# Embedding product moved behind the output projection, parked in DRAM; whole tiles in the residual

## Chip, cores, metric

One core of a Trainium2 chip (trn2) runs the whole block in one launch. The metric is the device time of that launch in microseconds, the median of several runs.

## The reference

One layer (DEPTH = 1), 512 positions, 1024 channels, everything in float32; cut to what the change touches:

```python
hn = rms_norm(h, g_mix_pre)
# three mixers and three sigmoid gates, each from hn @ w_in
merged = gates[:, :, 0] * br_a + gates[:, :, 1] * br_b + gates[:, :, 2] * br_c
h = h + rms_norm(merged @ w_out, g_mix_post)
hn = rms_norm(h, g_ffn_pre)
f_gate, f_up = jnp.split(hn @ w_ffn_in, 2, axis=-1)      # 1024 -> 2 x 2816
f = (jax.nn.silu(f_gate) * f_up) @ w_ffn_out             # 2816 -> 1024
h = h + rms_norm(f, g_ffn_post)
h = h + jax.nn.sigmoid(h @ w_ple_gate) * (p @ w_ple)     # p: 512 x 256
```

`rms_norm(x, g)` is x * rsqrt(mean(x * x) + 1e-6) * g over the channels. The embedding's product is `p @ w_ple`; it depends on nothing that the block computes.

## The kernel before

Channels lie on the 128 partitions, positions (512, or halves of 256) along the free axis; 1024 channels are 8 k-blocks (KT), a hidden size of 2816 is 22 (FT). Each float32 operand is split into a high part (rounded to fp32r by ACT) and a low part (the rest, by DVE), and a product of one k-block is three matmuls into one PSUM bank: high weights by high and by low activations, low weights by high activations (`mm3`; `product` runs the k-blocks of one tile, `product_k_outer` one k-block for several tiles in turn). A tile of 8 k-blocks is thus 24 matmuls.

**Weights** come through class `Weights`: `add` lists the blocks in order, `_next` issues the load on SP (a `raw` tile of 512 KB, 3 buffers), the cast on ACT (`hi`) and the subtraction on DVE (`lo`); `get` takes the next block and `ahead(n)` prepares blocks until n are ready. A block with no tag goes into the 3 stream buffers of `hi` and of `lo`; one with a tag goes into slots of the activations' pool that are free at the time ("tm" 6, "br", "hn" and "cv" 8 each, named `w_hi` and `w_lo`). A slot is taken again when the last reader of what it held is done.

**Order.** All operations of PE, ACT and DVE go through the helper `InOrder.engine.call` (L69 before, L71 after), so every row of the profile has that line and is told apart by the names of its tiles. Inside `with order():` each engine keeps the order in which the program is written; elsewhere a scheduler orders it. An engine runs its instructions strictly in order. Seven PSUM banks ("ps") are shared by all products, an eighth ("pst", `ps_stat`) holds the statistics.

**The stages around the change**, in order: the conv branch's projection (`ps_br`); the **output projection** (`ps_o`, `mix_tile`): tiles 0 to 3 with all 512 positions, 4 to 7 first for the left half, then for the right, each copied with its gain to `o_all` and squared by ACT, the squares summed into `o_sums` by DVE (`add_mixed`). Then per half `inv_rms`: a matmul pair with `mean_mat` gives the mean, `rsqrt` is eight dependent DVE operations (`o_inv`). `Residual.tile(k)` follows: DVE multiplies `o_all` by it and adds to `h_all`; ACT writes the high part of the scaled `h_all` (`hg`), DVE the low part, which is held back until the next tile's multiplication is issued (`flush` for the last). `square_h` and `add_h` sum the squares of the new `h_all` into `h_sums`.

The first six **feed-forward blocks** (2 * `N_PAIR`, six banks `ps_f`) run with k outermost, left half, then right; ahead of the right half's last k (`STAT_H` = 7) comes the statistic of `h_sums` for `h_inv`. From then on each block is a whole tile (`ffn_tile`) and `swiglu` multiplies each pair by `h_inv` out of PSUM. ffn_out (`ps_fo`, 8 tiles of 22 k-blocks in cuts of 8, 7 and 7) ends with tile 7 in halves; `evacuate` copies to `o2_all` and sums squares into `f_sums`. Then come, before the change, the **embedding's product** (`ps_ple`, `ple_tile`: 8 tiles of 6 matmuls, its copies kept in SBUF in slots "br") and beside it the residual of the left half, then the **gate product** (`ps_pg`): four blocks (`N_LAST`) with k outermost by halves, the others as whole tiles but for the last, and `finish`: sigmoid, multiplication by the embedding, sum, and the write of the output.

```python
def residual_ffn(hs):
    y = t2("f_inv", H)
    inv_rms(f_sums[:, hs], y)
    return Residual(o2_all, hs, y, h2, lambda k: 1.0)
```

Of the kernel before, what the change touches and what calls it, by code (L numbers as in the profile page):

```python
# [8 lines left out]
F32 = mybir.dt.float32  # L9
# [3 lines left out]
AF = mybir.ActivationFunctionType  # L13
# [3 lines left out]
P = 128  # L17
# [64 lines left out]
def hybrid_block(  # L82
# [16 lines left out]
    stat = ctx.enter_context(tc.tile_pool(name="stat", bufs=2))  # L99
    psum = ctx.enter_context(tc.tile_pool(name="psum", bufs=7, space=PSUM))  # L100
# [106 lines left out]
    def mm3(out, wh, wl, xh, xl, first, last):  # L207
        pe.matmul(out, lhsT=wh, rhs=xh, start=first, stop=False)
        pe.matmul(out, lhsT=wh, rhs=xl, start=False, stop=False)
        pe.matmul(out, lhsT=wl, rhs=xh, start=False, stop=last)  # L210
# [4 lines left out]
    def product(ps, w, acts, hs=FULL, k0=0, last=True):  # L215

        hi, lo = w
        for i, a in enumerate(acts):
            mm3(ps[:, hs], blk(hi, i), blk(lo, i), a[:, 0, hs], a[:, 1, hs],
                k0 + i == 0, last and i == len(acts) - 1)  # L220
# [65 lines left out]
    N_HALF = 4  # L286
    N_PAIR = 3

    def add_mix(*blocks):
        for b in blocks:  # L290
            weights.add(w_mix[b])
# [401 lines left out]
    def mix_tile(n, w, hs):  # L693
        ps = bank("ps_o")
        product(ps, w, mix_T, hs)
        act_e.activation(out=o_all[:, n, hs], in_=ps[:, hs], func=AF.Copy, scale=col("g_mix_post", n))
        if n == 0:
            act_e.activation(out=o_sums[:, hs], in_=ps[:, hs], func=AF.Square)
            return None
        return square(ps[:, hs], "o_sq")  # L700
# [16 lines left out]
    lo_half, hi_half = HALVES  # L717
    with order():
        for n in range(KT - N_HALF):
            sq = mix_tile(n, weights.get(2), FULL)  # L720
            add_mixed(sq, n, FULL)
            weights.ahead((5, 7, 9, 10)[n])
        late = [weights.get(0) for _ in range(N_HALF)]
        blocks = [weights.get(0) for _ in range(2 * N_PAIR)]
        for i in range(N_HALF):
            n = KT - N_HALF + i
            add_mixed(mix_tile(n, late[i], lo_half), n, lo_half)
        sqs = []
        for i in range(N_HALF):
            n = KT - N_HALF + i  # L730
            sq = mix_tile(n, late[i], hi_half)
            if i == 0:
                y = t2("o_inv", H)
                inv_rms(o_sums[:, lo_half], y)
                res = Residual(o_all, lo_half, y, hg, ffn_gain)
            sqs.append((sq, n))
            for k in MIX_CUT[i]:
                res.tile(k)
                if sqs:
                    add_mixed(*sqs.pop(0), hi_half)  # L740
        res.flush()


        banks = [bank("ps_f") for _ in range(2 * N_PAIR)]
        product_k_outer(banks, blocks, hg, lo_half, range(STAT_A))
        for k in range(KT):
            square_h(k, lo_half)
            add_h(k, lo_half, nc.gpsimd)
        y = t2("o_inv", H)
        inv_rms(o_sums[:, hi_half], y)  # L750
        res = Residual(o_all, hi_half, y, hg, ffn_gain)
        for k in range(KT):
            res.tile(k)
            if k > 1:
                add_h(k - 2, hi_half, dve)
            if k:
                square_h(k - 1, hi_half)
        res.flush()
        square_h(KT - 1, hi_half)
        add_h(KT - 2, hi_half, dve)  # L760
        add_h(KT - 1, hi_half, dve)
# [53 lines left out]
    ple = [slot("br", f"ple{i}", F32) for i in range(4)]  # L815

    def ple_tile(n, w, p):
        ps = bank("ps_ple")
        for k in range(2):
            s = slice((2 * (n % 4) + k) * P, (2 * (n % 4) + k + 1) * P)  # L820
            ts = slice(k * T, (k + 1) * T)
            mm3(ps, w[0][:, s], w[1][:, s], p[0][:, ts], p[1][:, ts], k == 0, k == 1)
        act_e.copy(ple[n // 2][:, n % 2], ps)
# [12 lines left out]

    with order():
        ps = bank("ps_fo")
        halves = [bank("ps_fo") for _ in HALVES]
        ffn_out(ps, KT - 2, 0, weights.get(2))  # L840
        w = weights.get(1)
        for b, hs in zip(halves, HALVES):
            ffn_out(b, KT - 1, 0, w, hs)
        w = weights.get(1)
        ffn_out(ps, KT - 2, 1, w)
        weights.ahead(3)
        w = weights.get(2)
        ffn_out(ps, KT - 2, 2, w)
        p_w, w_ple_0 = weights.get(0), weights.get(0)
        weights.ahead(3)  # L850
        evacuate(ps, KT - 2, FULL)
        last = [weights.get(0), weights.get(0)]
        weights.ahead(3)
# [7 lines left out]
        product(halves[1], (hi[:, 3 * P:], lo[:, 3 * P:]), f_T[c0 + 3:c1], hi_half, c0 + 3, False)  # L861
        ffn_out(halves[1], KT - 1, 2, last[1], hi_half)
        evacuate(halves[1], KT - 1, hi_half)


        w_ple_1 = weights.get(0)
        blocks = [weights.get(0) for _ in range(2)]
        k = 0
        for n in range(KT):
            ple_tile(n, w_ple_1 if n >= 4 else w_ple_0, p_w)  # L870
            while n > 0 and k < PLE_CUT[n - 1]:
                res.tile(k)
                k += 1
            if n == PLE_SPLIT:
                weights.ahead(2)
        blocks += [weights.get(0) for _ in range(2)]
        res.flush()
        banks = [bank("ps_pg") for _ in range(N_LAST)]
# [5 lines left out]
        product_k_outer(banks, blocks, h2, lo_half, range(STAT_F, KT))  # L884
        product_k_outer(banks, blocks, h2, hi_half)
        weights.ahead(2)
        for n in range(N_LAST):
            finish(banks[n], n, FULL)
        for n in range(N_LAST, KT):
# [71 lines left out]
```

## Time and profile before

| | |
|---|---|
| median of 3 runs | 984.22 us (984.08 to 984.52) |
| the profiled execution | 983.63 us, of which span 981.9 us |
| PE, DVE, ACT, POOL busy | 973.8, 677.3, 346.1, 88.2 us |
| conv branch's projection | 468.68 to 512.20 us |
| output projection | 512.20 to 557.41 us |
| first six feed-forward blocks | 557.41 to 593.07 us |
| end of ffn_out, embedding's product, gate product | to 921.47, to 932.37, to the end |

The span is what the profiler records between the first and the last instruction of the core; the time of the execution is longer by what lies around it. A busy PE in these rows is one with matmuls in flight: their ends are modelled, so the start of one to the start of the next is the better measure of a matmul. Where an engine was idle ahead of an instruction, its row names in brackets for how long and which engine's work ended it.

### The profile page before, as it was taken

The page shows a single profiled execution, that of the slowest core. Times are in us where ns is not written, and L with a number is a line of the kernel's source. Part 1 is how long each engine was busy: PE and PEld are TensorE (multiplying, and loading weights), DVE is VectorE, ACT ScalarE, POOL GpSimd, SP SyncE. Part 2 cuts the span into 40 slices and gives each one's busy share as a digit, 9 for nine tenths or more (in the row PEclk, how much of TensorE's full clock was granted, in tenths as well). Part 3 has the DMA queues.
Part 4 walks back from the last instruction along what each step waited for, and adds up shares of the span by engine and source line. Part 5 has one row for each costly group of instructions (what it writes and reads, how often), then busy time and mean ns, then how long its engine had stood idle before and what let it go on. Part 6 is the DMA issues. An engine that isn't in the chain of part 4 may idle for free.

```text
span 981.9 us, 11718 instructions
## 1 busy us (share of the span) xinstructions
PE 973.8 (99%) x4682; PEld 819.2 (83%) x4682; DVE 677.3 (69%) x903; ACT 346.1 (35%) x483; POOL 88.2 (9%) x64
## 2 busy tenths in 40 slices
PE   9999999999999999999999999999999999999998
PEld 6788888788888878888888998888888888888897
DVE  7898789999988899957555787544444432223575
ACT  6422333332224332146435443323232322223442
POOL 4000004000013712160000010000000000000000
PEclk9999999999999999999999999999999999999999
DMA  6433331323322322332338112323322333334312
GB/s 233 137 108 107 109 106 65 107 69 104 107 81 81 101 103 86 105 110 68 126 96 272 62 38 74 104 90 104 98 96 93 98 91 104 92 92 139 109 43 86
DMA packets 30006, 100.53 MB, mean 102 GB/s; under 512 B 3456, under 2 KB 3968, under 8 KB 29952
## 3 DMA queue, kind: packets, MB, share of 16 engines
q1 hardware_dynamic: 29808, 99.75, 30.9%
q8 instruction: 36, 0.59, 0.2%
q14 instruction: 18, 0.15, 0.0%
q10 hardware_dynamic: 144, 0.04, 0.0%
HBM read 97.68 MB, written 2.10 MB: 102 GB/s over the span
## 4 chain that ended last, share of the span: by engine, by line
PE 88%; DVE 7%; issue 2%; DMA 1%; ACT 1%; SPq 0%; DVEq 0%; ACTq 0%
PE ps_f L69 25%; PE ps_br L69 13%; PE ps_fo L69 12%; PE ps_gate L69 12%; PE ps_ag L69 5%; PE ps_pg L69 5%; PE ps_o L69 5%; PE ps_z L69 4%; PE ps_nat L69 4%; DVE lo L69 2%; DVE acc L69 2%; PE ps_ple L69 1%; PE ps_pool L69 1%; DVE v_all L69 1%; DMA first_all<-in_w_first 1%
## 5 line engine op out<-in xcount | busy, mean ns | idle before, releaser
L69 ACT CAST hi<-raw 128x1024 fp32r<-128x1024 f32 (+3 forms) x158 | 162.5, 1030 | 456.3 <-PE ps_br L69 88.4
L69 DVE TENSOR_TENSOR lo<-raw,hi 128x1024 fp32r<-128x1024 f32 (+3 forms) x158 | 206.2, 1306 | 107.0 <-ACT hi L69 106.5
L69 DVE SCALAR_TENSOR_TENSOR acc<-h_conv,vec,acc 128x511 f32<-128x511 f32 (+14 forms) x240 | 183.3, 764 | 5.2
L69 PE MATMUL ps_f<-hg,hi 128*128 128x512 f32 (+1 forms) x624 | 184.5, 379 | 0.0
L69 PEld LDWEIGHTS ps_f<-hg,hi 128*128 128x128 f32 x624 | 115.1, 188 | 21.7
L69 PE MATMUL ps_gate<-hn,hi 128*128 128x512 f32 x384 | 119.6, 392 | 0.9 <-DVE gated L69 0.9
L69 PE MATMUL ps_f<-hg,lo 128*128 128x512 f32 (+1 forms) x312 | 118.0, 379 | 0.0
L69 PE MATMUL ps_fo<-f,hi 128*128 128x512 f32 (+1 forms) x396 | 111.0, 366 | 0.0
L69 PEld LDWEIGHTS ps_gate<-hn,hi 128*128 128x128 f32 x384 | 72.0, 188 | 17.1 <-DVE gated L69 1.3
L69 PEld LDWEIGHTS ps_fo<-f,hi 128*128 128x128 f32 x396 | 71.7, 189 | 12.2
L69 PE MATMUL ps_nat<-hi,hn 128*128 128x512 f32 x256 | 78.8, 390 | 0.0
L69 PE MATMUL ps_gate<-hn,lo 128*128 128x512 f32 x192 | 74.9, 390 | 0.0
L69 PE MATMUL ps_fo<-f,lo 128*128 128x512 f32 (+1 forms) x198 | 72.5, 366 | 0.0
L69 PEld LDWEIGHTS ps_f<-hg,lo 128*128 128x128 f32 x312 | 58.7, 188 | 11.0
L69 PEld LDWEIGHTS ps_nat<-hi,hn 128*128 128x128 f32 x256 | 48.1, 188 | 10.0
L69 DVE TENSOR_TENSOR f<-ps_f,h_inv 128x512 f32<-128x512 f32 x22 | 15.2, 690 | 56.5 <-PE ps_f L69 56.5
L69 PE MATMUL ps_nat<-lo,hn 128*128 128x512 f32 x128 | 49.9, 390 | 0.0
L69 PE MATMUL ps_ag<-hn,hi 128*128 128x512 f32 x160 | 49.6, 391 | 0.2 <-DVE sig L69 0.2
L69 PEld LDWEIGHTS ps_fo<-f,lo 128*128 128x128 f32 x198 | 37.4, 189 | 6.0
L69 PEld LDWEIGHTS ps_gate<-hn,lo 128*128 128x128 f32 x192 | 36.1, 188 | 7.5
L69 DVE TENSOR_TENSOR silu<-ps_f,h_inv 128x512 f32<-128x512 f32 x22 | 15.2, 690 | 36.0 <-PE ps_f L69 35.9
L69 PE MATMUL ps_br<-pool,hi 128*128 128x512 f32 x128 | 39.6, 389 | 0.0
(214 smaller groups left out, 1566.5 us busy)
## 6 DMA issues: line engine op xcount, KB each, us to landing
raw<-in_w_mix SPq DMA_DIRECT2D x90, 512.0 KB, 3.2
raw<-in_w_ffn_in SPq DMA_DIRECT2D x44, 512.0 KB, 3.3
raw<-in_w_ffn_out SPq DMA_DIRECT2D x16, 448.0 KB, 3.3
raw<-in_w_ffn_out SPq DMA_DIRECT2D x8, 512.0 KB, 3.5
raw<-in_w_ple_gate SPq DMA_DIRECT2D x8, 512.0 KB, 4.2
x_all<-in_xT SPq DMA_DIRECT2D x8, 256.0 KB, 6.4
h_all<-in_xT SPq DMA_DIRECT2D x4, 512.0 KB, 5.2
out_dram<-pg SPq DMA_DIRECT2D x7, 256.0 KB, 2.0
```

Source lines behind the costliest of these rows:

```text
L69: inst = op(*args, **kw)
```

## The change

- The output projection runs all 8 tiles whole. Behind it the 8 tiles of the embedding's product run; ACT copies each to a temporary tile `ple_out`, from which SP's queue writes it to a DRAM tile `ple_dram`. At the end of ffn_out four loads of 512 KB on SP's queue bring them back into slots "br" and "tm".
- The statistic of `o_sums` comes after the second embedding tile (`PLE_STAT`). The residual and the first six feed-forward blocks run in whole tiles; all additions into `h_sums` are DVE's (the left half's were POOL's).
- The weights for this (`pT`, two of `w_ple` in slots "tm", and the six feed-forward blocks) are listed between the output projection's blocks (`N_LATER`), with more blocks ahead (`AHEAD_OUT`). Feed-forward blocks 6 to 8, in slots "tm" before, now use the stream's buffers.
- ffn_out's tile 6 runs its last cut in halves, the left one first; the `f_sums` statistic of the left half now has four k-blocks of tile 6's right half ahead of it, not three of tile 7's. `evacuate` and `mix_tile` issue the square ahead of the copy.
- Two further gate blocks (`N_MORE`) run by halves, each on its own; the gate's blocks 0 to 3 go into slots "hn".

```diff
+AHEAD_OUT = (2, 2, 3, 4, 4, 5, 5, 4)
+N_LATER = (0, 0, 0, 1, 1, 1, 2, 4)
...
+    later = [(pT, "tm"), (w_ple[0], "tm"), (w_ple[1], "tm")]
+    later += [(w_ffn_in[b], "br" if b < 4 else None) for b in range(2 * FT)]
     for n in range(KT):
-        weights.add(w_mix[S_OUT + n], "tm" if KT - N_HALF <= n < KT - 1 else None)
-    for b in range(2 * FT):
-        weights.add(w_ffn_in[b], "br" if b < 4 else "tm" if 6 <= b < 9 else None)
+        add_mix(S_OUT + n)
+        for _ in range(N_LATER[n]):
+            weights.add(*later.pop(0))
+    for item in later:
+        weights.add(*item)
...
+    def ple_tile(n, w, p):
...
+        t = t2("ple_out")
+        act_e.copy(t, ps)
+        nc.sync.dma_start(out=ple_dram[:, n], in_=t)
...
     with order():
...
+        late = []
+        for n in range(KT):
+            w = weights.get(0)
+            weights.ahead(AHEAD_OUT[n])
+            late += [weights.get(0) for _ in range(N_LATER[n])]
+            add_mixed(mix_tile(n, w, FULL), n, FULL)
+        p_w, *w_ple_hl = late[:3]
+        for n in range(KT):
+            if n == PLE_STAT:
+                y = t2("o_inv")
+                inv_rms(o_sums, y)
+                res = Residual(o_all, FULL, y, hg, ffn_gain)
+            ple_tile(n, w_ple_hl[n // 4], p_w)
+        blocks = late[3:]
...
         for k in range(KT):
             res.tile(k)
             if k > 1:
-                add_h(k - 2, hi_half, dve)
+                add_h(k - 2, FULL, dve)
...
+        banks = [bank("ps_f") for _ in range(2 * N_PAIR)]
+        product_k_outer(banks, blocks, hg, FULL, range(STAT_H))
         weights.ahead(2)
-        product_k_outer(banks, blocks, hg, lo_half, range(STAT_A, KT))
-        product_k_outer(banks, blocks, hg, hi_half, range(STAT_H))
         inv_rms(h_sums, h_inv)
-        product_k_outer(banks, blocks, hg, hi_half, range(STAT_H, KT))
+        product_k_outer(banks, blocks, hg, FULL, range(STAT_H, KT))
...
+        ffn_out(ps, KT - 2, 2, w_last, lo_half)
+        evacuate(ps, KT - 2, lo_half)
...
         for c in (1, 2):
-            ffn_out(halves[0], KT - 1, c, last[c - 1], lo_half)
+            ffn_out(halves[0], KT - 1, c, late[c - 1], lo_half)
         evacuate(halves[0], KT - 1, lo_half)
-        c0, c1 = ffn_out_cuts[1]
-        hi, lo = last[0]
-        product(halves[1], (hi, lo), f_T[c0:c0 + 3], hi_half, c0, False)
+        c0, c1 = ffn_out_cuts[2]
+        product(ps, w_last, f_T[c0:c0 + 4], hi_half, c0, False, skip_group_check=True)
         res = residual_ffn(lo_half)
...
+        for i in range(4):
+            nc.sync.dma_start(out=ple[i], in_=ple_dram[:, 2 * i:2 * i + 2])
...
+        res.tile(0)
+        evacuate(ps, KT - 2, hi_half)
+        res.tile(1)
         evacuate(halves[1], KT - 1, hi_half)
...
         product_k_outer(banks, blocks, h2, lo_half, range(STAT_F))
+        more = [weights.get(1) for _ in range(N_MORE)]
         res = residual_ffn(hi_half)
```

How the change moves instructions at three places. **DVE around the inverse root of `h_sums`**: `h_sums`, `h_inv` and `rs_t` are rows of 512, `w_lo` and `lo` are the low parts of feed-forward weights. Before:

```order
L69 TENSOR_TENSOR h_sums<-h_sums,o_all 128x256 [waits DVE_49,Activation_49] x2
L69 TENSOR_TENSOR w_lo<-raw,w_hi 128x1024 [waits DMAHW6_49,Activation_49]
L69 TENSOR_TENSOR w_lo<-raw,w_hi 128x1024 [waits DMAHW7_49,Activation_49]
L69 TENSOR_SCALAR h_inv<-ps_stat 128x512 [waits PE_49]
L69 TENSOR_TENSOR rs_t<-h_inv 128x512 [waits DVE_49]
L69 SCALAR_TENSOR_TENSOR rs_t<-rs_t,ps_stat 128x512 [waits DVE_49]
L69 SCALAR_TENSOR_TENSOR h_inv<-rs_t,h_inv 128x512 [waits DVE_49]
L69 TENSOR_TENSOR rs_t<-h_inv 128x512 [waits DVE_49]
L69 TENSOR_TENSOR rs_t<-rs_t,ps_stat 128x512 [waits DVE_49]
L69 SCALAR_TENSOR_TENSOR rs_t<-rs_t 128x512 [waits DVE_49]
L69 SCALAR_TENSOR_TENSOR h_inv<-rs_t,h_inv 128x512 [waits DVE_49]
```

And now:

```order
L71 TENSOR_TENSOR h_sums<-h_sums,o_all 128x512 [waits DVE_49,Activation_49] x2
L71 TENSOR_TENSOR lo<-raw,hi 128x1024 [waits DMAHW1_49,Activation_49]
L71 TENSOR_TENSOR lo<-raw,hi 128x1024 [waits DMAHW2_49,PE_49,Activation_49]
L71 TENSOR_SCALAR h_inv<-ps_stat 128x512
L71 TENSOR_TENSOR rs_t<-h_inv 128x512 [waits DVE_49]
L71 SCALAR_TENSOR_TENSOR rs_t<-rs_t,ps_stat 128x512 [waits DVE_49]
L71 SCALAR_TENSOR_TENSOR h_inv<-rs_t,h_inv 128x512 [waits DVE_49]
L71 TENSOR_TENSOR rs_t<-h_inv 128x512 [waits DVE_49]
L71 TENSOR_TENSOR rs_t<-rs_t,ps_stat 128x512 [waits DVE_49]
L71 SCALAR_TENSOR_TENSOR rs_t<-rs_t 128x512 [waits DVE_49]
L71 SCALAR_TENSOR_TENSOR h_inv<-rs_t,h_inv 128x512 [waits DVE_49]
L71 TENSOR_TENSOR silu<-ps_f,h_inv 128x512 [waits DMAHW4_49,DMAHW0_49,DVE_49]
```

The two splits ahead of `h_inv` go from slots of their own to the stream's, and the second of them now also waits for PE.

**ACT at the passage from the output projection to the feed-forward blocks**: `o_sq` is the square of an output tile, `hg` with a number the scaled residual of one channel block. Before, at the last half tiles:

```order
L69 ACTIVATE o_sq<-ps_o 128x256 [waits DVE_49]
L69 ACTIVATE o_all<-ps_o,vec 128x256 [waits PE_49]
L69 ACTIVATE o_sq<-ps_o 128x256 [waits DVE_49]
L69 ACTIVATE hg_3837<-h_all,vec 128x256 [waits DVE_49]
L69 ACTIVATE o_all<-ps_o,vec 128x256 [waits PE_49]
L69 ACTIVATE o_sq<-ps_o 128x256 [waits Activation_49]
L69 ACTIVATE hg_3838<-h_all,vec 128x256 [waits DVE_49]
L69 ACTIVATE hg_3839<-h_all,vec 128x256 [waits DVE_49]
L69 ACTIVATE o_all<-ps_o,vec 128x256 [waits PE_49]
L69 ACTIVATE o_sq<-ps_o 128x256 [waits Activation_49]
```

And now:

```order
L71 CAST hi<-raw 128x1024 [waits DMAHW0_49,DVE_49]
L71 ACTIVATE o_sq<-ps_o 128x512 [waits PE_49]
L71 ACTIVATE o_all<-ps_o,vec 128x512
L71 COPY ple_out<-ps_ple 128x512 [waits PE_49] x2
L71 COPY ple_out<-ps_ple 128x512 [waits DVE_49,PE_49] x2
L71 COPY ple_out<-ps_ple 128x512 [waits DMAHW4_49,PE_49,Activation_49]
L71 COPY ple_out<-ps_ple 128x512 [waits DMAHW5_49,PE_49,Activation_49]
L71 COPY ple_out<-ps_ple 128x512 [waits DMAHW6_49,PE_49,Activation_49]
L71 COPY ple_out<-ps_ple 128x512 [waits DMAHW7_49,PE_49,Activation_49]
L71 ACTIVATE hg_3839<-h_all,vec 128x512 [waits DVE_49]
L71 ACTIVATE hg_3840<-h_all,vec 128x512 [waits DVE_49]
```

The copies of the embedding's tiles stand between the last output tile and the first `hg`, where before `hg` came between the output's half tiles.

**DVE behind the left half's `f_inv`**: `h_0` and `h_1` are the low parts of the residual's first two blocks. Before:

```order
L69 SCALAR_TENSOR_TENSOR f_inv<-rs_t,f_inv 128x256 [waits DVE_49]
L69 TENSOR_TENSOR f_sums<-f_sums,sq 128x256 [waits Activation_49]
L69 TENSOR_TENSOR o_all<-o_all,f_inv 128x256 [waits DVE_49]
L69 TENSOR_TENSOR h_all<-h_all,o_all 128x256 [waits DVE_49]
L69 TENSOR_TENSOR o_all<-o_all,f_inv 128x256
L69 SCALAR_TENSOR_TENSOR h_0_6078<-h_all,h_0_6078 128x256 [waits Activation_49]
L69 TENSOR_TENSOR h_all<-h_all,o_all 128x256 [waits DVE_49]
L69 TENSOR_TENSOR o_all<-o_all,f_inv 128x256
L69 SCALAR_TENSOR_TENSOR h_1_6079<-h_all,h_1_6079 128x256 [waits Activation_49]
L69 TENSOR_TENSOR h_all<-h_all,o_all 128x256 [waits DVE_49]
L69 TENSOR_TENSOR w_lo<-raw,w_hi 128x1024 [waits DMAHW1_49,PE_49,Activation_49]
L69 TENSOR_TENSOR w_lo<-raw,w_hi 128x1024 [waits DMAHW2_49,PE_49,Activation_49]
```

And now:

```order
L71 SCALAR_TENSOR_TENSOR f_inv<-rs_t,f_inv 128x256 [waits DVE_49]
L71 TENSOR_TENSOR o_all<-o_all,f_inv 128x256 [waits DVE_49]
L71 TENSOR_TENSOR h_all<-h_all,o_all 128x256 [waits DVE_49]
L71 TENSOR_TENSOR f_sums<-f_sums,sq 128x256 [waits Activation_49]
L71 TENSOR_TENSOR o_all<-o_all,f_inv 128x256
L71 SCALAR_TENSOR_TENSOR h_0_5860<-h_all,h_0_5860 128x256 [waits DVE_49]
L71 TENSOR_TENSOR h_all<-h_all,o_all 128x256 [waits DVE_49]
L71 TENSOR_TENSOR f_sums<-f_sums,sq 128x256 [waits Activation_49]
L71 TENSOR_TENSOR o_all<-o_all,f_inv 128x256
L71 SCALAR_TENSOR_TENSOR h_1_5861<-h_all,h_1_5861 128x256 [waits DVE_49]
L71 TENSOR_TENSOR h_all<-h_all,o_all 128x256 [waits DVE_49]
L71 TENSOR_TENSOR o_all<-o_all,f_inv 128x256
```

The second addition into `f_sums` now stands in the residual too, each ahead of a low part, and the two weight splits that followed are gone from here.

## Rows read from the trace of the kernel before

**Rows 1.** The page: engines (1) and the chain of waits (4).

```profile
PE 973.8 (99%) x4682; PEld 819.2 (83%) x4682; DVE 677.3 (69%) x903; ACT 346.1 (35%) x483; POOL 88.2 (9%) x64
...
PE 88%; DVE 7%; issue 2%; DMA 1%; ACT 1%; SPq 0%; DVEq 0%; ACTq 0%
```

**Rows 2.** Waits of PE, the longest after the start: us, times, longest.

```profile
PE ps_gate L69 <- DVE gated L69: 0.9, 1, 0.9
```

**Rows 3.** The chain in order of time: start us, us, what.

```profile
468.68 43.52 PE ps_br L69 x192
...
562.16 28.07 PE ps_f L69 x234
590.23 0.86 PE ps_stat L69 x2
...
921.47 10.91 PE ps_ple L69 x48
```

**Rows 4.** Timeline of PE at 590 and 916 us: start us, us, instruction.

```profile
590.06 1.02 PE L69 MATMUL ps_stat<-h_sums,mean_mat 128*128 128x512 f32 x2
...
916.31 0.28 PE L69 MATMUL ps_fo<-f,lo 128*128 128x256 f32 x1
916.81 0.70 PE L69 MATMUL ps_stat<-f_sums,mean_mat 128*128 128x256 f32 x2 [0.23 <-DVE f_sums L69]
917.16 0.47 PE L69 MATMUL ps_fo<-f,hi 128*128 128x256 f32 x1
```

**Rows 5.** Timeline of DVE from 591 us, full width.

```profile
591.12 0.69 DVE L69 TENSOR_SCALAR h_inv<-ps_stat 128x512 int32<-128x512 int32 x1 [5.17 <-PE ps_stat L69]
...
596.99 0.69 DVE L69 TENSOR_TENSOR silu<-ps_f,h_inv 128x512 f32<-128x512 f32 x1
```

**Rows 6.** Timeline of DVE at 917 and 943 us, half width.

```profile
917.55 0.43 DVE L69 TENSOR_SCALAR f_inv<-ps_stat 128x256 int32<-128x256 int32 x1 [0.79 <-PE ps_stat L69]
...
920.76 0.42 DVE L69 SCALAR_TENSOR_TENSOR f_inv<-rs_t,f_inv 128x256 f32<-128x256 f32 x1
...
943.72 0.42 DVE L69 TENSOR_TENSOR o_all<-o_all,f_inv 128x256 f32<-128x256 f32 x1
...
944.97 0.42 DVE L69 TENSOR_TENSOR o_all<-o_all,f_inv 128x256 f32<-128x256 f32 x1
```

**Rows 7.** Timeline of ACT at 924 us.

```profile
924.25 0.59 ACT L69 COPY ple<-ps_ple 128x512 f32<-128x512 f32 x1 [0.77 <-PE ps_ple L69]
924.73 0.42 ACT L69 ACTIVATE h<-h_all 128x256 fp32r<-128x256 f32 x1
```

**Rows 8.** Groups of ACT by form: xcount, busy us, mean ns, idle us.

```profile
L69 ACT CAST w_hi<-raw 128x1024 fp32r<-128x1024 f32 x17 | 17.5, 1048 | 9.9 <-DMA raw<-in_w_ffn_in 3.9 <-DMA raw<-in_w_mix 2.8 <-PE ps_fo L69 2.5
...
L69 ACT ACTIVATE xg<-x_all,vec 128x512 fp32r<-128x512 f32 x8 | 5.8, 721 | 0.9 <-DMA x_all<-in_xT 0.9
...
L69 ACT ACTIVATE sq<-ps_fo 128x256 f32<-128x256 f32 x2 | 0.8, 377 | 0.0
```

**Rows 9.** A group of DVE by form, same columns.

```profile
L69 DVE TENSOR_TENSOR w_lo<-raw,w_hi 128x1024 fp32r<-128x1024 f32 x17 | 20.6, 1224 | 11.4 <-ACT w_hi L69 8.9 <-PE ps_fo L69 2.5
```

**Rows 10.** Timeline of PE in the first 10 us.

```profile
1.33 3.59 PE L69 MATMUL ps_warm<-warm_up 128*128 128x512 bf16 x8 [1.33 <-DVE warm_up L69]
5.49 4.71 PE L69 MATMUL ps_first<-xg,first 128*128 128x512 f32 x12 [0.57 <-ACT first L69]
```

**Rows 11.** Windows: length; busy PE, PEld, DVE, ACT, POOL; clock, DMA share, GB/s.

```profile
186.50:188.50 2.00, 1.09 (x5) 0.62 (x4) 2.00 (x4) 1.80 (x4) 0.00 (x0) 1.00 0.12 20
512.20:557.41 45.21, 45.21 (x292) 41.42 (x292) 28.00 (x43) 23.52 (x38) 0.00 (x0) 1.00 0.57 187
0.00:10.00 10.00, 8.11 (x20) 4.64 (x21) 4.88 (x11) 6.68 (x12) 0.79 (x7) 1.00 0.79 257
```

**Rows 12.** The page, DMA issues: xcount, KB each, median us to landing.

```profile
raw<-in_w_ple_gate SPq DMA_DIRECT2D x8, 512.0 KB, 4.2
...
out_dram<-pg SPq DMA_DIRECT2D x7, 256.0 KB, 2.0
```

More of the change, by code (lines that the diff above doesn't have):

```diff
@@ L205, in hybrid_block, with mm3, product @@
     weights = Weights()
[L207 to L210, printed above, removed]
+    def mm3(out, wh, wl, xh, xl, first, last, **kw):
+        pe.matmul(out, lhsT=wh, rhs=xh, start=first, stop=False, **kw)
+        pe.matmul(out, lhsT=wh, rhs=xl, start=False, stop=False, **kw)
+        pe.matmul(out, lhsT=wl, rhs=xh, start=False, stop=last, **kw)
     def blk(w, k):
         return w[:, k * P:(k + 1) * P]
-    def product(ps, w, acts, hs=FULL, k0=0, last=True):
+    def product(ps, w, acts, hs=FULL, k0=0, last=True, **kw):
         hi, lo = w
@@ L285, in hybrid_block @@
     S_SGU, S_CONV, S_POOL, S_OUT = 64, 72, 80, 88
-    N_HALF = 4
     N_PAIR = 3
@@ L695, in mix_tile @@
         product(ps, w, mix_T, hs)
-        act_e.activation(out=o_all[:, n, hs], in_=ps[:, hs], func=AF.Copy, scale=col("g_mix_post", n))
+        sq = None
         if n == 0:
             act_e.activation(out=o_sums[:, hs], in_=ps[:, hs], func=AF.Square)
-            return None
-        return square(ps[:, hs], "o_sq")
+        else:
+            sq = square(ps[:, hs], "o_sq")
+        act_e.activation(out=o_all[:, n, hs], in_=ps[:, hs], func=AF.Copy, scale=col("g_mix_post", n))
+        return sq
     def add_mixed(sq, n, hs):
@@ L715, in add_h @@
             add_sq(h_sums[:, hs], o_all[:, k, hs], k, engine)
-    lo_half, hi_half = HALVES
-    with order():
[L719 to L751, printed above, removed]
@@ L814, in hybrid_block @@
         evacuate(ps, n, FULL)
[L815 to L823, printed above, removed]
+    lo_half, hi_half = HALVES
     def residual_ffn(hs):
@@ L843, in hybrid_block @@
             ffn_out(b, KT - 1, 0, w, hs)
-        w = weights.get(1)
-        ffn_out(ps, KT - 2, 1, w)
         weights.ahead(3)
[L847 to L853, printed above, removed]
+        ffn_out(ps, KT - 2, 1, weights.get(2))
+        weights.ahead(4)
+        w_last = weights.get(0)
+        late = [weights.get(0)]
@@ L854, in hybrid_block @@
+        blocks = [weights.get(0) for _ in range(2)]
+        weights.ahead(1)
+        ffn_out(ps, KT - 2, 2, w_last, lo_half)
+        evacuate(ps, KT - 2, lo_half)
+        late.append(weights.get(0))
+        weights.ahead(2)
         for c in (1, 2):
-            ffn_out(halves[0], KT - 1, c, last[c - 1], lo_half)
+            ffn_out(halves[0], KT - 1, c, late[c - 1], lo_half)
         evacuate(halves[0], KT - 1, lo_half)
-        c0, c1 = ffn_out_cuts[1]
-        hi, lo = last[0]
-        product(halves[1], (hi, lo), f_T[c0:c0 + 3], hi_half, c0, False)
+        c0, c1 = ffn_out_cuts[2]
@@ L876, in hybrid_block @@
-        blocks += [weights.get(0) for _ in range(2)]
+        product(ps, [w[:, 4 * P:] for w in w_last], f_T[c0 + 4:c1], hi_half, c0 + 4,
+                skip_group_check=True)
+        for c in (1, 2):
+            ffn_out(halves[1], KT - 1, c, late[c - 1], hi_half)
+        ple = [slot("br" if i < 2 else "tm", f"ple{i}", F32) for i in range(4)]
+        for i in range(4):
+            nc.sync.dma_start(out=ple[i], in_=ple_dram[:, 2 * i:2 * i + 2])
+        blocks += [weights.get(0) for _ in range(2)]
@@ L884, in hybrid_block @@
         product_k_outer(banks, blocks, h2, lo_half, range(STAT_F, KT))
+        for ps, w in zip(banks[N_LAST:], more):
+            product(ps, w, h2, lo_half)
         product_k_outer(banks, blocks, h2, hi_half)
+        for ps, w in zip(banks[N_LAST:], more):
+            product(ps, w, h2, hi_half)
         weights.ahead(2)
-        for n in range(N_LAST):
-            finish(banks[n], n, FULL)
-        for n in range(N_LAST, KT):
+        for n, ps in enumerate(banks):
+            finish(ps, n, FULL)
+        for n in range(len(banks), KT):
             w = weights.get()
```

57 lines of the change are left out of this document (24 added, 33 removed).

## The prediction

> **What bounds the kernel now.** The page first [rows 1]: PE is busy for 973.8 of 981.9 us, DVE for 677.3, ACT for 346.1, and the chain of waits gives PE 88%. So the time is the matmuls, and a change can help in two ways only: fewer or cheaper matmuls, or less idle time of PE. The waits of PE show how little of the second there is: after the start the longest is 0.9 us [rows 2], and in the stages that the change touches the one that shows is 0.2 us at the f_sums statistic [rows 4]. The chain in order of time [rows 3] then gives the stages and the price of a matmul: in the conv branch's projection 192 whole ones (512 columns) take 43.52 us, 0.2267 each; among the feed-forward blocks 234 of half width take 28.07 us, 0.1200 each. Two halves cost 0.0132 more than one whole. From 468 us to the end PE is fed without a break. What the halves buy stands in the order of the work: while PE does one half, DVE does the eight-step inverse root of the other. The question is what covers that chain when the tiles are whole.
>
> **Matmuls.** The last four output tiles become whole (96 pairs merged, 96 x 0.0132 = 1.27 us less), and so do six feed-forward blocks (144 pairs, 1.90 less). Split are the last cut of ffn_out's tile 6 (7 k-blocks x 3 = 21, 0.28 more) and two gate blocks (48, 0.64 more). The wait at f_sums (0.50 us from 916.31 to 916.81 where a half matmul takes 0.12 [rows 4]) should go: tile 7's sums now have four k-blocks of cover instead of three, and the square comes ahead of the copy; 0.38 less. Together -2.64.
> Beside this stands a rule of the Trainium skill, page "TensorE: Matmul & The Clock Gate", section "Back-to-back issue gap": a matmul has a fixed part of some 2.5 ns, so the net 171 merges would give 0.43 us by it. The trace disagrees, 13 ns against 2.5, and the sum goes by the trace.
>
> **Stall 1: embedding to feed-forward.** The output projection starts at 512.20 as before and takes 8 x 24 x 0.2267 = 43.5 us; two embedding tiles of 1.364 (10.91/8 [rows 3]) follow, so the o_sums statistic starts at X = 558.44. On PE: two matmuls, 0.86, and six tiles, 8.18: free at 567.5. On DVE: the inverse root starts 1.06 after the statistic's start (590.06 to 591.12 [rows 4, 5]), its eight steps take 5.87 to the next operation (591.12 to 596.99 [rows 5]), multiplication and add some 1.4 more: h_all of tile 0 is there at 566.8. But ACT works in its order, and the copy of embedding tile 7 stands ahead of hg of tile 0. It starts when PE ends tile 7 (567.55, with 0.06 that I take for the handover), the next ACT operation follows 0.48 later (924.25 to 924.73 [rows 7]), hg takes 0.72 (the xg row of the same form [rows 8]): 568.75. The low half on DVE takes about a step of the chain, 0.73 (5.87 / 8), and ends at 569.5, the second matmul needs it and would have run at 567.7. So +1.9 us; 1.6 if the handovers are shorter, 2.1 if each costs 0.1 more. A gain is excluded, as PE has nothing else in its queue.
>
> **Stall 2: the second whole feed-forward tile.** Let U be the start of the h_sums statistic. PE: 0.87, then k=7 of six blocks, 18 x 0.2267 = 4.08, then block 6 in the seventh bank, 5.44: at U+10.4 it asks for the bank of block 0, free once DVE has multiplied h_inv into it. Before, the inverse root began 1.06 after the statistic, ended 5.87 later and the multiplication 0.69 later [rows 5]: that would be U+7.6, in time. Now two weight splits stand ahead of it on DVE, as before; but blocks 6 to 8 have lost their own slots and take the stream's. Block 7 takes the slot of block 4, which PE leaves only with the 14th of those 18 matmuls, at U+4.05. Cast on ACT 1.05, low part on DVE 1.22 [rows 8, 9]: U+6.4 with the handovers, and h_inv behind it. Chain 5.87, multiplication 0.69: U+12.94, a stall of 2.55. I take +2.7, with 0.05 on each of three handovers; 2.4 if they cost nothing and the cast starts a little sooner, 3.0 with 0.15 on each. The tiles after it have their splits in time by the same prices.
>
> **Stall 3: ffn_out to the gate.** W is the start of the f_sums statistic of the left half. PE: 0.35 (916.81 to 917.16 [rows 4]), 51 half matmuls, 6.12; at W+6.5 it turns to the gate product, whose second matmul, at W+6.65, needs the low part of h2 tile 0. Before, the embedding's 10.91 us covered this. DVE: 0.74 to the first step (916.81 to 917.55), eight steps 3.67 (917.55 to 920.76, and 0.42 for the last [rows 4, 6]): o_all at W+4.4, h_all ends W+5.25. ACT: high part 0.42 [rows 7], and only then the square of tile 6's right half, 0.38 [rows 8]: W+6.05. DVE adds that square and multiplies o_all of tile 1, 0.34 apart, ahead of the low part, which ends at W+7.15: 0.5 us. Tile 1 is the same with tile 7's square, W+9.38 against W+8.6: 0.77. After that DVE needs 1.25 per tile (943.72 to 944.97 [rows 6]) and PE 12 x 0.12 = 1.44: covered. For the right half three gate splits stand ahead of the inverse root on DVE: the left half's low parts end at W+16.9 (six more at 1.25), three splits of 1.22 to W+20.5, eight steps to W+24.2, then o_all, h_all, high part, the next o_all and the low part as above, W+26.2. PE comes there at W+25.6 (W+6.65, 144 half matmuls or 17.3, the statistic's 0.35, the 1.27 just found): 0.6. Together, with their restarts, +2.0; 1.5 if two handovers are shorter, 2.6 if each costs 0.2 more.
>
> **Costed at nothing.** The embedding's product itself, 48 matmuls, only moves. Its copies and three more weight splits lie in a stretch where ACT is busy for 23.5 and DVE for 28 of 45.2 us and the DMA engines for 0.57 [rows 11]; if that cover failed, the price would be one split, 1.05 + 1.22. The eight writes to DRAM (2.0 us of a like kind) and four reads back (4.2 us for 512 KB [rows 12]) are some 350 us apart. On SP the reads stand behind the load of the last gate block but one, which waits for DVE's gate splits, that is until about W+20; four reads end to end would be there at W+37, and the first finish comes at W+41 at the earliest, 288 half matmuls after W+6.5. Behind them stands only the load of the last gate block, wanted after one more whole block. If this cover went too, each late read would cost up to 4.2. On SP the load of pT goes ahead of the four loads of h_all, which is wanted only beside the residual at 566. The h_sums adds that POOL did go to DVE beside 8 tiles of matmuls. The tail is as before.
>
> **The sum.** -2.64 + 1.9 + 2.7 + 2.0 = +4.0. The profiled execution took 983.63 us (981.9 of span and 1.7 around it), 0.59 below the median of 984.22: 987.6 against it, 988.2 against the median. By the bounds +2.9 to +5.1: 987.1 to 989.3.
>
> **Rivals.**
> *Block 7's split does not hold h_inv* (not slower). If the slot is left by U+1.5, the low part ends by U+3.8, the chain meets U+10.4 and stall 2 is gone: 988.2 - 2.7 = 985.5, within 984.6 and 986.4. For it speaks that the same pair of splits stood at the same place before without a wait; against it the order, where the second now waits for PE. 0.12.
> *No stall at all*: the engines' handovers are far quicker than the rows, or another cover exists that I missed: only the matmuls count, 984.2 - 2.6 = 981.6. Stall 1 has a chain of four dependent operations after PE's last product, which speaks against. 0.06.
> *The clock falls.* The first 20 matmuls of the program, after idle time, take 3.59 and 4.71 us [rows 10] where 20 x 0.2267 = 4.5: 3.8 more. If the 2.7 us of stall 2 brought the same on, 988.2 + 3.8 = 992.0. Against it: the break of 0.9 us at 188 us [rows 2] lies in a stretch with PE busy for 1.09 of 2.00 us, and the granted clock stayed 1.00 there, that is 2.4 GHz; it reads 1.00 in the first 10 us too, so those slow matmuls are a bound and no more [rows 11]. 0.07. The Trainium skill, same page, section on the clock gate, says that an idle array falls to half clock; no row here shows it after a break as short as these.
> *Merging saves nothing*: if a whole matmul took here what two halves take, the 3.17 saved by merges and the 0.92 spent on splits both go: 988.2 + 2.25 = 990.4. The rows of both widths speak against it, 0.2267 against twice 0.1200. 0.05. By the fixed part of 2.5 ns on the page of the Trainium skill named above it would be 990.0.
>
> **How the numbers follow.** My forecast, all three stalls, has 0.70. A measurement of this kernel can tell 0.2%, 1.97 us: under 982.25 is faster, over 986.19 slower. Slower: nearly all of the forecast (0.68), the clock and the merges (0.12): 0.80. The same: the first rival but for a tenth, 0.11, 0.02 of the forecast, 0.01 of the second: 0.14. Faster: the rest of the second and a remnant, 0.06. The range of 985.0 to 990.2 holds the forecast, most of the first rival and half of the last; it leaves out no stalls and the clock.
>
> **What would show it.** Right: PE waits for hg on ACT or DVE near 568 (1.9), for h_inv or silu after block 6 (2.7) with DVE's weight split just ahead of h_inv, and two or three waits of 0.5 to 0.8 in the first gate blocks; ps_o and the first ps_f in rows of 0.227 per matmul; no wait at f_sums. Wrong: a PE as busy as before, h_inv starting within 2 us of its statistic, or a long wait for weights in the output projection, whose margin I have only from busy times.

## The result, and the profile after

The changed kernel takes 989.72 us (median of 5, 988.58 to 990.26) against 984.52 for the kernel before (984.08 to 984.94): ratio 1.005, 95% interval 1.0036 to 1.0063. It is slower, by 5.2 us where 4.0 were forecast. The profiled execution is the one of 989.72 us, with a span of 987.9 against 981.9.

The page, engines and chain of waits [rows 1]: PE has 173 matmuls fewer and its share of the chain falls from 88 to 84%, while DVE's rises from 7 to 10 and ACT's from 1 to 2.

```profile
PE 974.5 (99%) x4509; PEld 810.0 (82%) x4509; DVE 672.3 (68%) x867; ACT 342.9 (35%) x461; POOL 83.5 (8%) x58
...
PE 84%; DVE 10%; issue 3%; ACT 2%; DMA 1%; SPq 0%; DVEq 0%; ACTq 0%
```

The waits of PE (line and releaser: total, times, longest) are in the first half of the program within 0.2 us those of before. In the second half there are four new ones, of which the first is the longest of all:

```profile
PE ps_f L71 <- DVE silu L71: 2.5, 1, 2.5
PE ps_f L71 <- ACT hg L71: 1.3, 1, 1.3
...
PE ps_pg L71 <- DVE h L71: 0.8, 2, 0.5
...
PE ps_f L71 <- DVE hg L71: 0.3, 1, 0.3
```

In the second half of the program the chain in order of time (start, length, what) leaves PE at three places, of which these rows, the counterpart of [rows 3], show the first two:

```profile
470.27 43.52 PE ps_br L71 x192
513.79 43.52 PE ps_o L71 x192
...
560.04 0.86 PE ps_stat L71 x2
560.90 8.19 PE ps_ple L71 x36
569.15 0.59 ACT ple_out L71
569.74 0.63 ACT hg L71
570.39 0.76 DVE hg L71
571.20 28.64 PE ps_f L71 x125
599.84 0.86 PE ps_stat L71 x2
600.70 3.21 PE ps_f L71 x14
603.92 1.06 ACT hi L71
605.01 1.23 DVE lo L71
606.24 0.61 DVE h_inv L71
...
611.94 0.70 DVE silu L71
612.78 201.57 PE ps_f L71 x888
```

Read it from the top. The output projection runs without a break, 192 whole matmuls in 43.52 us. The statistic of `o_sums` starts, the other six embedding tiles follow, and then the chain leaves PE: the copy of the last tile (569.15), `hg` behind it on ACT, the low part on DVE, and PE again at 571.20. The second place starts with the statistic of `h_sums` at 599.84: after 14 matmuls the chain goes to a cast on ACT (603.92), to the weight split on DVE (605.01), and only then begins `h_inv` (606.24), 6.4 us after the statistic, where before it took 0.9 (590.23 to 591.12 [rows 3, 5]). PE is back at 612.78. The third place is at the passage to the gate product, here by DVE's timeline (start, length, instruction, and in brackets the idle time before it and its releaser):

```profile
933.67 0.43 DVE L71 TENSOR_TENSOR h_all<-h_all,o_all 128x256 f32<-128x256 f32 x1
934.85 0.43 DVE L71 TENSOR_TENSOR f_sums<-f_sums,sq 128x256 f32<-128x256 f32 x1 [0.76 <-ACT sq L71]
...
935.53 0.42 DVE L71 SCALAR_TENSOR_TENSOR h<-h_all,h 128x256 fp32r<-128x256 f32 x1
...
937.04 0.43 DVE L71 TENSOR_TENSOR f_sums<-f_sums,sq 128x256 f32<-128x256 f32 x1 [0.76 <-ACT sq L71]
...
946.12 3.50 DVE L71 TENSOR_TENSOR lo<-raw,hi 128x1024 fp32r<-128x1024 f32 x3 [0.52 <-ACT hi L71]
949.54 0.42 DVE L71 TENSOR_SCALAR f_inv<-ps_stat 128x256 int32<-128x256 int32 x1
...
954.56 0.42 DVE L71 SCALAR_TENSOR_TENSOR h<-h_all,h 128x256 fp32r<-128x256 f32 x1
```

`f_sums` waits 0.76 us twice for a square that stands behind `hg`'s counterpart `h` on ACT (the first `h` starts at 934.13, its square at 934.45), and each time the low part comes after it; further down three weight splits, 3.5 us together, stand directly ahead of `f_inv`. PE's timeline shows what that costs, and that the wait at the `f_sums` statistic is gone (928.80 to 928.92, where [rows 4] has 0.50 us):

```profile
928.80 0.28 PE L71 MATMUL ps_fo<-f,lo 128*128 128x256 f32 x1
928.92 0.59 PE L71 MATMUL ps_stat<-f_sums,mean_mat 128*128 128x256 f32 x2
...
936.00 0.39 PE L71 MATMUL ps_pg<-h,w_hi 128*128 128x256 f32 x1 [0.27 <-DVE h L71]
...
938.19 0.39 PE L71 MATMUL ps_pg<-h,w_hi 128*128 128x256 f32 x1 [0.49 <-DVE h L71]
...
954.58 0.84 PE L71 MATMUL ps_pg<-h,w_hi 128*128 128x256 f32 x2
```

Taken from start to start, less the 0.227 or 0.120 us that a matmul takes, the three places cost 2.17, 2.71 and 1.87 us: 6.75. (The third consists of 0.53, 0.75 and 0.59.) With the -2.64 of the matmuls and of `f_sums` that is +4.11. From the start of the 192 matmuls of the conv branch's projection to the start of the last matmul of the program the trace has 509.13 us before and 513.29 after: +4.16. This **length** is the measure for the experiments. Of the rest of the 6.0 us of span, 1.6 lie ahead of it, in a half of the program that PE, DVE and ACT run in the same order in both kernels. The other 0.3 lie behind it: from the start of the last matmul to the end of the span it is 4.51 us, where before it was 4.21.

### The profile page after: what moved, and what is told of

Same layout as the page of the kernel before. It is cut to its first block, busy times and chain, and to the rows that moved or that the text cites. A ratio compares the mean times of both kernels' runs of the same rounds, so it can differ in the third digit from the quotient of the medians.

```text
span 987.9 us, 11336 instructions
## 1 busy us (share of the span) xinstructions
PE 974.5 (99%) x4509; PEld 810.0 (82%) x4509; DVE 672.3 (68%) x867; ACT 342.9 (35%) x461; POOL 83.5 (8%) x58
## 4 chain that ended last, share of the span: by engine, by line
PE 84%; DVE 10%; issue 3%; ACT 2%; DMA 1%; SPq 0%; DVEq 0%; ACTq 0%
PE ps_f L71 24%; PE ps_br L71 13%; PE ps_gate L71 12%; PE ps_fo L71 12%; PE ps_ag L71 5%; PE ps_z L71 4%; PE ps_o L71 4%; PE ps_nat L71 4%; PE ps_pg L71 3%; DVE lo L71 2%; DVE acc L71 2%; DVE rs_t L71 1%; PE ps_ple L71 1%; PE ps_pool L71 1%; DVE v_all L71 1%
## 5 line engine op out<-in xcount | busy, mean ns | idle before, releaser
L71 ACT CAST hi<-raw 128x1024 fp32r<-128x1024 f32 (+3 forms) x163 | 167.6, 1031 | 480.5 <-PE ps_br L71 88.4
L71 DVE TENSOR_TENSOR lo<-raw,hi 128x1024 fp32r<-128x1024 f32 (+3 forms) x163 | 212.1, 1303 | 133.0 <-ACT hi L71 132.7
L71 PE MATMUL ps_f<-hg,hi 128*128 128x512 f32 x640 | 196.9, 389 | 2.5 <-DVE silu L71 2.5
L71 PEld LDWEIGHTS ps_f<-hg,hi 128*128 128x128 f32 x640 | 120.0, 188 | 27.9 <-issue 2.9
L71 PE MATMUL ps_f<-hg,lo 128*128 128x512 f32 x320 | 124.3, 389 | 0.0
```

Source lines behind the costliest of these rows:

```text
L71: inst = op(*args, **kw)
```

## The experiments

| kernel | conv projection starts | last matmul starts | length | half-rate matmuls in it | median us |
|---|---|---|---|---|---|
| before | 468.51 | 977.64 | 509.13 | none | 984.52 |
| before, once more | 470.33 | 979.45 | 509.12 | none | 985.43 (one run) |
| changed | 470.11 | 983.40 | 513.29 | none | 989.72 |
| changed, once more | 469.78 | 984.67 | 514.89 | 8 | 990.96 (one run) |
| own slots for blocks 6 to 8 | 470.35 | 980.80 | 510.45 | none | 986.57 |
| block 7 behind the inverse root | 469.63 | 980.10 | 510.47 | none | 987.62 |
| `hg` 0 ahead of the last copy | 470.22 | 983.69 | 513.47 | 8 | 989.41 |
| statistic after the first tile | 468.75 | 983.91 | 515.16 | 8 | 990.15 |
| squares out of the way | 469.83 | 983.17 | 513.34 | 8 | 989.54 |
| one gate split out of the way | 469.92 | 984.23 | 514.32 | 8 | 989.86 |
| a third split ahead of `h_inv` | 468.99 | 984.85 | 515.86 | 6 | 991.64 |
| all four repairs | 469.76 | 976.49 | 506.73 | none | 982.45 |

Starts are those of PE's matmuls in each profile. Half-rate matmuls start 0.427 us after one another instead of 0.227. They are told of at the end of the section; a set of eight costs 1.6 us of length, the set of six 1.4.

**Stall 2, by the slots.**

```diff
-    later += [(w_ffn_in[b], "br" if b < 4 else None) for b in range(2 * FT)]
+    later += [(w_ffn_in[b], "br" if b < 4 else "tm" if 6 <= b < 9 else None) for b in range(2 * FT)]
```

> Measure, here and in the later runs: the length from the start of the conv branch's projection to the start of the last matmul (changed kernel 513.1 us, kernel before 509.0), and PE's wait at the place in question. Theory (block 7 takes block 4's stream slot, its split waits for PE and stands ahead of h_inv): with slots of their own for feed-forward blocks 6 to 8 the wait after block 6 (2.7 us) is gone, length 510.4. Rival (a whole tile behind six banks has to wait for the bank anyway, whatever the slots): the wait stays at 2.7.

Measured: no wait behind block 6, length 510.45. On DVE `h_inv` now follows its statistic (599.91 on PE) after 1.06 us, as before:

```profile
600.97 0.69 DVE L71 TENSOR_SCALAR h_inv<-ps_stat 128x512 int32<-128x512 int32 x1 [9.60 <-PE ps_stat L71]
```

Ratio to the kernel before 1.0021 (1.0012 to 1.0031). The rival is out: with the splits done early, six banks and a seventh are enough.

**Stall 2, by the order.**

```diff
-        weights.ahead(2)
+        weights.ahead(1)
         inv_rms(h_sums, h_inv)
+        weights.ahead(2)
```

> Only block 7's weights are prepared behind the inverse root of h_sums instead of ahead of it; the slots stay as in the changed kernel. Theory: the split still waits for PE, but h_inv no longer stands behind it, so the first multiplication ends some 9 us after the statistic, ahead of PE at 10.4: wait 2.7 to 0, length 510.4. Rival (the wait for the bank is set by the chain itself or by the first split): 1.2 at most is gained, the work of one split, wait 1.5 or more.

Measured: no wait, length 510.47. The split of block 7 still takes the stream's slot, but stands behind the eight steps, and the multiplication that frees the bank ends at 607.8, 8.6 us after the statistic's start at 599.20 on PE:

```profile
605.33 0.69 DVE L71 SCALAR_TENSOR_TENSOR h_inv<-rs_t,h_inv 128x512 f32<-128x512 f32 x1
605.94 1.22 DVE L71 TENSOR_TENSOR lo<-raw,hi 128x1024 fp32r<-128x1024 f32 x1
607.08 0.68 DVE L71 TENSOR_TENSOR silu<-ps_f,h_inv 128x512 f32<-128x512 f32 x1
```

So it was not the split's work that cost 2.7 us, but its wait for PE, passed on through DVE's order.

**Stall 2, made larger.**

```diff
-        weights.ahead(2)
+        weights.ahead(3)
         inv_rms(h_sums, h_inv)
```

> A third weight split (block 8, in block 5's stream slot) is put ahead of the inverse root of h_sums, nothing else: the suspected cause made larger. Theory (a split that waits for PE stands ahead of h_inv on DVE): block 5's slot is left three matmuls later and DVE has 1.2 us more to do, so the wait after block 6 grows from 2.7 to 3.9; rival (the bank's release is set by the chain alone): stays at 2.7. Second question, the granted clock: the runs so far show eight or so matmuls at 0.427 instead of 0.227 us behind some of the long waits, 1.6 us together, not behind others. If a longer wait decides it, they stand behind this wait of 3.9; if it is chance, perhaps not.

Measured: PE's break (start to start) grows from 2.93 to 4.08 us, less 0.23 a wait of 3.85. In the list of waits:

```profile
PE ps_f L71 <- DVE silu L71: 3.7, 1, 3.7
```

The rival, by which the wait would have stayed at 2.7, is out. The ratio to the kernel before is 1.0077 (1.006 to 1.0094); part of that is the clock, below.

**Stall 1, by ACT's order.** `res.tile(0)` is called behind embedding tile 6, ahead of tile 7:

```diff
             ple_tile(n, w_ple_hl[n // 4], p_w)
+            if n == 6:
+                res.tile(0)
...
         for k in range(KT):
-            res.tile(k)
+            if k:
+                res.tile(k)
```

> hg of block 0 goes ahead of the copy of the last embedding tile on ACT, nothing else. Theory (ACT's order): hg is written at the end of h_all of block 0 instead of behind the copy; what is left is DVE's low part, which comes behind the next multiplication: the wait of 2.1 falls to 0.6 to 0.9, length 511.8. Rival (DVE's chain behind the statistic sets the start): no change, wait 2.1.

Measured: 0.81 us is left of 2.17. ACT's timeline has `hg` ahead of the copy that held it:

```profile
568.39 0.72 ACT L71 ACTIVATE hg<-h_all,vec 128x512 fp32r<-128x512 f32 x1
569.26 0.59 ACT L71 COPY ple_out<-ps_ple 128x512 f32<-128x512 f32 x1 [0.15 <-ACT hg L71]
```

The length is 513.47 with eight half-rate matmuls, 511.9 without their 1.6. The ratio, 1.0044 (1.0029 to 1.0059), does not tell this from the changed kernel; the trace does.

**Stall 1, the rival's repair.**

```diff
-STAT_K, STAT_H, STAT_F, PLE_STAT = 4, 7, 2, 2
+STAT_K, STAT_H, STAT_F, PLE_STAT = 4, 7, 2, 1
```

> The statistic of o_sums comes after the first embedding tile instead of the second, nothing else. Theory (ACT's order): DVE is 1.36 us earlier, but the copy of the last embedding tile still stands ahead of hg of block 0, so the wait stays at 2.0 to 2.1, length 513.1 (0.1 to 0.3 more if the statistic now waits for o_sums). Rival (DVE's chain sets it): wait 0.7, length 511.8.

Measured: the wait stays at 2.12, and 0.3 is added at the statistic, which now waits for `o_sums`. DVE has `h_all` of block 0 at 565.75, its low part starts at 569.32:

```profile
565.06 0.69 DVE L71 TENSOR_TENSOR h_all<-h_all,o_all 128x512 f32<-128x512 f32 x1
...
569.32 0.75 DVE L71 SCALAR_TENSOR_TENSOR hg<-h_all,vec,hg 128x512 fp32r<-128x512 f32 x1 [2.96 <-ACT hg L71]
```

In between ACT copies the last embedding tile, and `hg` follows:

```profile
568.08 0.58 ACT L71 COPY ple_out<-ps_ple 128x512 f32<-128x512 f32 x1 [0.73 <-PE ps_ple L71]
568.56 0.72 ACT L71 ACTIVATE hg<-h_all,vec 128x512 fp32r<-128x512 f32 x1
```

DVE's chain is not what sets the start. Alone, an earlier statistic is worth less than nothing.

**Stall 3, the squares.** `evacuate` of tile 6's right half goes ahead of `res.tile(0)`; tile 7's square is issued behind `res.tile(1)`, its sum and copy behind `res.tile(2)`:

```diff
-        res.tile(0)
         evacuate(ps, KT - 2, hi_half)
+        res.tile(0)
         res.tile(1)
-        evacuate(halves[1], KT - 1, hi_half)
-        for k in range(2, KT):
+        sq = square(halves[1][:, hi_half])
+        res.tile(2)
+        add_sq(f_sums[:, hi_half], sq, KT - 1, dve)
...
+        for k in range(3, KT):
             res.tile(k)
```

> The squares of the right halves move out of the way of the low parts in the left half's residual: tile 6's square and sum ahead of the residual, tile 7's square behind the high part of block 1 and its sum behind block 2's add. Theory: the first two waits of the gate product (0.53 and 0.75 us with their restarts) go to 0.1 or less each, the third, at the right half (0.59), stays: length 511.9. Rival (the chain of the left half is simply too long for the cover of 51 half matmuls): both waits stay, or the second grows by what the first loses.

Measured: the first two waits are gone without a remnant; the third falls too, from 0.59 to 0.30, which was not expected: DVE gained more here than PE. The rival, a chain too long for its cover, is out. Without the half-rate matmuls the length is 511.7.

**Stall 3, the splits.**

```diff
-        more = [weights.get(1) for _ in range(N_MORE)]
+        more = [weights.get(n) for n in (1, 0)]
...
             res.tile(k)
         res.flush()
+        weights.ahead(1)
```

> One of the three gate weight splits ahead of the right half's inverse root is moved behind the right half's residual. Theory: DVE is 1.2 us earlier there and the third wait (0.59) is gone, the first two stay: length 512.5. Rival (f_sums or the statistic come late, not the splits): no change.

Measured: the third wait is gone, the first two stand at 0.53 and 0.76; from the first gate matmul to the last 47.34 us instead of 47.94. Length without half-rate matmuls 512.7.

**All of it**: own slots for blocks 6 to 8, the statistic after the first embedding tile with `res.tile(0)` behind tile 5, the squares and the gate split.

> All together: own slots for blocks 6 to 8, statistic after the first embedding tile and hg of block 0 ahead of the copy of the last but one, squares and one gate split out of the way. Theory: none of the waits is left, 6.7 us less than the changed kernel: length 506.4, 2.6 less than the kernel before, the saving of the matmuls alone; median about 0.25% below the kernel before. Rival (a wait that is taken away comes back at the next place): length above 508, no faster than the kernel before.

Measured: 982.45 us (median of 11), ratio to the kernel before 0.998 (0.9971 to 0.9989); length 506.73. Of the waits of PE only those of the program's first half are left, seven rows, of which these are the first and the last:

```profile
PE ps_warm L71 <- DVE warm_up L71: 1.3, 1, 1.3
...
PE ps_mix L71 <- DVE v_split L71: 0.2, 1, 0.2
```

The chain of waits stays on PE from the statistic of `o_sums` on, where the changed kernel's left it at each of the three stalls:

```profile
558.38 1.13 PE ps_stat L71 x2
559.50 9.55 PE ps_ple L71 x42
569.06 28.57 PE ps_f L71 x126
...
598.48 210.82 PE ps_f L71 x930
```

The statistic itself still starts 0.2 us late, and its two matmuls take 0.1 more: 0.3 of the 0.33 that the length is over the expected one. This version beats both kernels. Its length is 2.40 us below that of the kernel before, nearly what the matmuls alone were worth; the median is 2.0 below (0.2%), as the 0.3 us behind the last matmul stay: 4.51 us to the end of the span here too.

**The two kernels once more.**

> The kernel before once more, for its profile: how much of the way to the conv branch's projection (468.5 us in its first profile, 468.8 to 470.4 in those of the changed kernels, whose first half is the same) changes from execution to execution. Theory: that spread lies in the waits and in the granted clock of the first 50 us and has nothing to do with the change: this profile may show any value from 468.5 to 470.5; from there on its length is 509.0 to 509.2 with no matmul at 0.427 us. Rival (the change makes the first half slower): 468.5 again.

Measured: the start of the projection moves by 1.8 us between two profiles of the same kernel, the length by 0.01. The two profiles of the kernel before (468.51 and 470.33) span about the range of the ten profiles of changed kernels, 468.75 to 470.35, so the 1.6 us by which the first half of the changed kernel's profile was later need no doing of the change. About half of them can be seen in the first 11 us: the matmuls go from 0.427 to 0.227 us apart at 9.1 us in the first profile of the kernel before, at 10.8 us in that of the changed kernel, which costs 0.8; the other 0.8 are lost in breaks of under 0.7 us between 40 and 48 us. In the profile of this run PE waits 1.8 us near 40 us and then runs slowly:

```profile
41.74 0.67 PE L69 MATMUL ps_ag<-hn,hi 128*128 128x512 f32 x1 [1.81 <-DVE hn L69]
```

> The changed kernel once more, for its profile. Theory: the three waits are the same to 0.1 us (2.1, 2.7 and 1.9), and the length from the start of the conv branch's projection is 513.1 to 513.4 without matmuls at 0.427 us behind a wait, 514.7 to 515.0 with eight of them. Rival (the lengths of 513.3 to 515.2 come from other operations): a length between, with waits of another size.

Measured: 514.89, with the three places at 2.17, 2.71 and 1.9 us and eight matmuls at half rate behind the first.

**The granted clock.** Matmuls at half rate stand in eight of the twelve profiles somewhere behind the first 39 us, in two of these at the start only. In windows (length, busy time and instructions of PE, PEld, DVE, ACT and POOL, then granted clock, DMA share, GB/s), the run with the squares moved, behind stall 2:

```profile
613.90:617.40 3.50, 3.50 (x10) 2.69 (x10) 2.07 (x3) 2.02 (x3) 0.00 (x0) 0.51 0.02 5
617.40:620.00 2.60, 2.60 (x13) 2.11 (x12) 2.43 (x4) 0.63 (x1) 0.00 (x0) 1.00 0.40 118
```

The granted clock is 0.51, that is 1.2 instead of 2.4 GHz, for one stretch that begins 1.4 us after PE went to work again, with ten matmul records in 3.5 us. In PE's timeline the matmuls go from 0.23 us apart (613.05 to 613.28) to 0.43 (614.77 to 615.20):

```profile
612.51 0.70 PE L71 MATMUL ps_f<-hg,hi 128*128 128x512 f32 x2 [2.55 <-DVE silu L71]
613.05 0.39 PE L71 MATMUL ps_f<-hg,lo 128*128 128x512 f32 x1
613.28 0.62 PE L71 MATMUL ps_f<-hg,hi 128*128 128x512 f32 x2
...
614.77 0.63 PE L71 MATMUL ps_f<-hg,lo 128*128 128x512 f32 x1
615.20 1.05 PE L71 MATMUL ps_f<-hg,hi 128*128 128x512 f32 x2
```

The changed kernel once more shows the same behind stall 1,

```profile
571.40:574.40 3.00, 3.00 (x8) 2.31 (x8) 2.62 (x6) 2.04 (x4) 0.00 (x0) 0.50 0.00 0
```

and the kernel before once more at its start, where it has such a break too:

```profile
42.20:45.20 3.00, 3.00 (x9) 2.31 (x8) 3.00 (x6) 0.41 (x1) 0.00 (x0) 0.50 0.00 0
```

Over all profiles, from 39 us on: after breaks of 1.68 us and more (from start to start of two matmuls) the clock fell 9 times of 20, after the 24 breaks of 1.2 to 1.3 us (two in each profile, at 188 and 350 us) never. The third split settles less than it was meant to: behind its break of 4.08 us the clock was at 0.50 at once (the window from 612.70 to 615.50, PE back at 612.82), but one profile cannot tell a rule from chance. What makes the clock fall behind one break of 2.93 us and not behind the next stays open. The Trainium skill, page "TensorE: Matmul & The Clock Gate", section "HAM oscillation — how this bites in real kernels", says that a matmul engine made to wait goes back to half clock and starts its next work slowly; the runs agree that half clock follows a wait. They differ in two things: it happened behind 9 of the 20 breaks only, and in six of these nine PE's first matmuls still ran at full rate, for about one to two us, before they slowed down. Where the slow matmuls lie in the length they cost 1.4 to 1.6 us.

## Why the prediction was right

The time lies in the forecast range, 985.0 to 990.2, on the side that had 0.80, and the three stalls are there. That the median lies inside is in part luck: two of the five executions (990.24 and 990.26) and the changed kernel once more (990.96) lie above the range, for the reason given last.

- **Matmuls and f_sums**, -2.64: with all stalls repaired the length is 2.40 below the kernel before, 2.7 without the 0.3 at the statistic that the repair itself brings. The price of a merge was right. The rule of the 2.5 ns from the Trainium skill, page "TensorE: Matmul & The Clock Gate", section "Back-to-back issue gap", by which the net merges save 0.43, and the rival in which they save nothing are both refuted by this run. The `f_sums` wait went as said.
- **Stall 1**, +1.9: 2.17, by the forecast mechanism. The copy, `hg` and low part start as worked out; the 0.3 more are handovers and the restart. That ACT's order and not DVE's chain decides was shown from both sides.
- **Stall 2**, +2.7: 2.71. The wait on block 4's slot, the cast, the split and the eight steps stand in the chain one after another; three runs (slots, order, a third split) move it as the step says. The rival in which the split does not hold `h_inv` is out.
- **Stall 3**, +2.0: 1.87, its three parts 0.53, 0.75 and 0.59 against 0.5, 0.77 and 0.6.
- **What cost nothing**: no row of the waits of PE names a DMA, a write or a read of the embedding's tiles; the output projection's 192 matmuls follow each other without a break in 43.52 us, so its weights came in time. One term put at nothing was not nothing: the tail was to be as before, but from the start of the last matmul to the end of the span it takes 4.50 to 4.52 us in all ten profiles of changed kernels, 4.21 in both of the kernel before. The output's last write ends 3.0 us after that start in either kernel, so the 0.3 lie behind it, in the end of the program; no experiment looks for their cause.
- **What was mis-sized** is the clock. The forecast put its fall into a rival of 0.07 and 3.8 us, taken from the 20 matmuls at the program's start [rows 10]. Of six profiles with both first stalls uncut, five show a fall, of 1.4 to 1.6 us each. One reading behind that small chance was wrong too: the 1.00 of the first 10 us [rows 11] says nothing of the slow matmuls there, as the trace's first record of the clock stands at 9.12 us; from 6.1 to 9.1 us the matmuls start 0.427 us after one another, as at half rate.

So the sum was made for an execution without a fall. By the measured length the median should have come out at 988.7 (984.52 and 4.16); it came out 1.0 higher. The tail is 0.3 of that. For the other 0.7 the executions differ: of the five, 988.58 has granted clock 1.00, and 990.24 and 990.26 have 0.998, which is what eight matmuls at half rate make of it. The profiled one, which is the median, has no fall, but a late start instead.

## What to carry to other kernels

Merging two half tiles saves 13 ns per matmul pair here, but halves are also what covers a chain on another engine: before merging, write out for each such chain what PE does meanwhile, instruction by instruction in every engine's own order. What stood in the way was small and not the chain itself: a copy ahead of the one urgent operation, a split that waits for a buffer ahead of an inverse root, a square ahead of a low part; each was put right by moving a few lines or by another slot, and then the change paid, by 0.2%. Give work that has to wait a place behind the urgent work of its engine, or a buffer that is free by then.

## What the runs showed of the hardware

That a wait of PE can cost more than its own length: behind breaks of 1.7 to 4.1 us the granted clock fell to half in 9 of 20 cases, and some eight matmuls of 512 columns then took 0.427 us each instead of 0.227, 1.6 us in all. And that the first 50 us of the program, with the time at which the matmuls first reach 0.227 us and with waits near 40 us, moved all that follows by 1.8 us between two profiles of the kernel before, while the length from the conv branch's projection on repeated within 0.01 us.
